# A feed-forward stage on one core: column tiles of the next chunk's first product between the pairs of the second, and more pairs by seven products

## The chip, the cores and the metric

The kernel runs on one core of one Trainium2 chip. The time is device microseconds of one launch; before the change the median of three runs was 1108.19 us (1107.41 to 1110.0). Smaller is better. The engines are PE (TensorE, the matrix unit; PEld is its weight load), DVE (VectorE), ACT (ScalarE), POOL (GpSimd) and SP (SyncE, which issues the transfers).

## The reference

One layer of an encoder: two batches of 128 tokens, width 2048. A mixer (two attentions and an output projection), a cross attention to a memory, and a feed-forward stage, each followed by a residual and a layer norm. The change lies wholly in the feed-forward stage:

```
def squared_relu_mlp(h, w_mlp_in, w_mlp_out):
    return jnp.square(jax.nn.relu(h @ w_mlp_in)) @ w_mlp_out

ff = squared_relu_mlp(x, w_mlp_in[l], w_mlp_out[l])
x = layer_norm(ALPHA * x + ff, ln3_g[l], ln3_b[l])
```

`w_mlp_in` is 2048 x 8192, `w_mlp_out` 8192 x 2048, all in fp32. The stage takes the time from about 400 us to 1096 us of the profiled execution.

## The kernel before

**Products in three.** Every fp32 operand is split into a part that the matrix unit takes at its reduced precision (hi) and the rest (lo): `split` lets ACT copy src to hi and DVE subtract to lo. A product is then three matmuls, hi x hi, hi x lo and lo x hi (`mm3`, lines 145 to 148). Weights come in blocks of 128 x 2048 fp32 (1 MB, "raw"), are split in parts of 1024 columns into buffers `w_hi` and `w_lo` (four of each), and are used once. So each part of weights costs one transfer, one ACT copy, one DVE subtraction, and the matmuls that read them.

**First product.** The 8192 hidden columns are four chunks of 16 tiles of 128. `hidden_group` makes four tiles at once in four PSUM banks: for each of 16 slices of the width, `cols_wide` issues four matmuls of 512 columns (weights hi times both parts of x, L195) and four of 256 (weights lo times x hi, L200). Per tile that is 16 of each. `hidden` and `square` evacuate the banks: ACT copies a half, DVE adds the other, takes relu and square in one operation (L823), and the result is split into `ht`.

**Second product.** The 2048 output columns are taken in two halves (q = 0, 1), so a chunk c has two passes (c, q). A pass accumulates over eight pairs of 128-row blocks of weights; the tokens are two blocks of 128. A plain pair is eight products (two row blocks, two column blocks of 512, two token blocks), 24 matmuls of 512 columns. A pair "by seven products" uses a Strassen-like identity in Winograd's form: 21 matmuls, for which DVE makes sums of the weight blocks (one operation over 1024 columns and two over 512, L886) and, once per chunk, sums of hidden blocks (four operations over 128 columns, then a split). The banks are x11, x12, x21, x22 and p1, p5, p6, p7; at the end of a pass they are combined and added to the residual `res` (L943, L946 from the banks, L949 from copies that ACT makes of the p banks). `SEVEN = ((2, 5, 7), (2, 5, 7))` names the pairs that go by seven. The last half pass, (3, 1), is plain and goes block by block (`proj_tokens` with `by_block`).

**Order.** A chunk's first product runs whole, then its two passes: the product of 16 tiles, 8 pairs, 8 pairs, next chunk. The program is written in Python in this order; a scheduler then sets each engine's order by dependence and priority, so engines may take work from a later place while buffers allow. Within an engine instructions run in the order that results. Side work (merges, statistics) stands in a queue `side`, of which `pump` takes an item after each part of weights. Weight sums stand in `sums`, taken in the same way, but the rest is flushed when the seven-product pair begins.

## Time and profile before

| | |
|---|---|
| median of three runs | 1108.19 us |
| profiled execution, span | 1106.6 us |
| mean granted PE clock | 0.997 |
| PE, DVE, ACT busy | 99%, 78%, 53% |
| first product of a chunk | 89.7 us |
| two passes of a chunk | 83.0 us |
| chunk 3's passes, the second plain | 86.0 us |
| after the last matmul | 10.5 us |

The time of a run is slightly more than the span, which begins with the first recorded instruction. A busy share is an average over the program. A line number stands for the code that issues an instruction, often a helper: L80 and L81 are the two operations of `split`, whoever calls it. The form `w_lo<-raw,w_hi 128x1024` names what is written and read, and the partitions and columns.

### The profile page before, as it was taken

How to read it: one execution, taken by the hardware profiler on the slowest of the kernel's cores; microseconds unless marked ns; L12 is line 12 of the kernel's file. 1: busy time of each engine (PE TensorE's matmuls, PEld its weight loads, DVE VectorE, ACT ScalarE, POOL GpSimd, SP SyncE). 2: the span in 40 equal slices, each digit the busy share in tenths (PEclk: the TensorE clock that was granted, in tenths of full speed). 3: DMA queues.
4: the chain of work that ended last, by engine and by line, in shares of the span. 5: the costliest groups of instructions: out<-in, count | busy, mean ns of one | idle time of the engine just before them, and what ended most of it. 6: DMA issues, size and time to landing. Idle time of an engine off the chain costs nothing.

```text
span 1106.6 us, 15304 instructions
## 1 busy us (share of the span) xinstructions
PE 1091.8 (99%) x5951; PEld 944.8 (85%) x5951; DVE 861.1 (78%) x1261; ACT 587.3 (53%) x860; POOL 35.6 (3%) x45
## 2 busy tenths in 40 slices
PE   9999999999999999999999999999999999999996
PEld 6988899988999878888888888888888888888885
DVE  6878677688879678888977678978668887678796
ACT  6455566545576435455655445555445555545550
POOL 1402000000100000000000000000000000000000
PEclk9999999999999999999999999999999999999998
DMA  9664453467567318744556555455554556555372
GB/s 333 234 227 142 156 193 127 174 220 247 180 205 272 145 44 299 266 166 181 192 223 221 184 185 209 181 200 192 198 183 175 204 200 223 186 191 190 115 255 87
DMA packets 37944, 215.86 MB, mean 195 GB/s; under 512 B 4336, under 2 KB 5232, under 8 KB 14192
## 3 DMA queue, kind: packets, MB, share of 16 engines
q1 hardware_dynamic: 37872, 214.89, 54.5%
q8 instruction: 46, 0.75, 0.3%
q14 instruction: 26, 0.21, 0.1%
HBM read 212.78 MB, written 2.10 MB: 194 GB/s over the span
## 4 chain that ended last, share of the span: by engine, by line
PE 98%; DVE 1%; DMA 0%; ACT 0%; issue 0%; POOL 0%; DVEq 0%; SPq 0%
PE acc L146 15%; PE acc L147 15%; PE acc L148 15%; PE acc L195 11%; PE att L195 11%; PE att L200 5%; PE acc L200 5%; PE att L147 3%; PE att L148 3%; PE att L146 3%; PE acc L188 2%; PE acc L186 2%; PE acc L187 2%; PE att L350 1%; PE acc L698 1%; PE att L528 1%
## 5 line engine op out<-in xcount | busy, mean ns | idle before, releaser
L81 DVE TENSOR_TENSOR w_lo<-raw,w_hi 128x1024 fp32r<-128x1024 f32 (+2 forms) x318 | 365.9, 1163 | 123.7 <-ACT w_hi L80 118.8
L80 ACT ACTIVATE w_hi<-raw 128x1024 fp32r<-128x1024 f32 (+2 forms) x318 | 317.9, 1011 | 266.0 <-PE acc L148 101.9
L80 ACT ACTIVATE w_hi<-wx 128x1024 fp32r<-128x1024 f32 x98 | 100.8, 1031 | 119.4 <-PE acc L148 85.5
L81 DVE TENSOR_TENSOR w_lo<-wx,w_hi 128x1024 fp32r<-128x1024 f32 x98 | 114.8, 1182 | 53.9 <-ACT w_hi L80 53.8
L195 PE MATMUL att<-x2t,w_hi 128*128 128x512 f32 x512 | 139.6, 394 | 0.0
L147 PE MATMUL acc<-w_lo,ht 128*128 128x512 f32 x354 | 137.8, 389 | 0.0
L148 PE MATMUL acc<-w_hi,ht 128*128 128x512 f32 x354 | 137.7, 389 | 0.0
L195 PE MATMUL acc<-x2t,w_hi 128*128 128x512 f32 x480 | 132.4, 394 | 0.0
L146 PE MATMUL acc<-w_hi,ht 128*128 128x512 f32 x354 | 111.5, 389 | 0.0
L195 PEld LDWEIGHTS att<-x2t,w_hi 128*128 128x128 f32 x512 | 88.0, 189 | 12.3
L195 PEld LDWEIGHTS acc<-x2t,w_hi 128*128 128x128 f32 x480 | 82.5, 189 | 11.5
L200 PEld LDWEIGHTS att<-x2t,w_lo 128*128 128x128 f32 x512 | 77.6, 189 | 10.3
L200 PEld LDWEIGHTS acc<-x2t,w_lo 128*128 128x128 f32 x480 | 73.3, 189 | 9.5
L200 PE MATMUL att<-x2t,w_lo 128*128 128x256 f32 x512 | 80.3, 281 | 0.0
L147 PEld LDWEIGHTS acc<-w_lo,ht 128*128 128x128 f32 x354 | 66.4, 188 | 14.0 <-DVE w_lo L81 0.2
L148 PEld LDWEIGHTS acc<-w_hi,ht 128*128 128x128 f32 x354 | 66.5, 188 | 13.8
L146 PEld LDWEIGHTS acc<-w_hi,ht 128*128 128x128 f32 x354 | 66.4, 188 | 13.8
L200 PE MATMUL acc<-x2t,w_lo 128*128 128x256 f32 x480 | 77.0, 281 | 0.0
L148 PE MATMUL acc<-w_hi,xt 128*128 128x512 f32 (+2 forms) x192 | 69.9, 365 | 0.0
L147 PE MATMUL acc<-w_lo,xt 128*128 128x512 f32 (+2 forms) x192 | 69.7, 364 | 0.0
L146 PE MATMUL acc<-w_hi,xt 128*128 128x512 f32 (+2 forms) x192 | 66.4, 366 | 0.8 <-ACT w_hi L80 0.8
L148 PE MATMUL acc<-w_hi,ot 128*128 128x512 f32 (+1 forms) x136 | 51.9, 382 | 0.0
(259 smaller groups left out, 1873.1 us busy)
## 6 DMA issues: line engine op xcount, KB each, us to landing
raw<-in_w_mi SPq DMA_DIRECT2D x64, 1024.0 KB, 4.9
wx<-in_w_mo SPq DMA_DIRECT2D x28, 1024.0 KB, 4.9
raw<-in_w_mo SPq DMA_DIRECT2D x28, 1024.0 KB, 4.8
raw<-in_w_out SPq DMA_DIRECT2D x16, 1024.0 KB, 4.9
raw<-in_w_ml SPq DMA_DIRECT2D x8, 1024.0 KB, 4.9
raw<-in_w_b SPq DMA_DIRECT2D x5, 1024.0 KB, 4.9
raw<-in_w_qa SPq DMA_DIRECT2D x16, 256.0 KB, 5.4
raw<-in_w_qa SPq DMA_DIRECT2D x4, 1024.0 KB, 4.8
```

The lines of the kernel that those rows point to most:

```text
L80: pin(nc.scalar.activation(hi, src, AF.Copy), pinned)
L81: return pin(nc.vector.tensor_tensor(out=lo, in0=src, in1=f(hi), op=ALU.subtract), pinned)
L146: nc.tensor.matmul(ps, ah, bh, start=start, stop=False)
L147: nc.tensor.matmul(ps, ah, bl, start=False, stop=False)
L148: nc.tensor.matmul(ps, al, bh, start=False, stop=stop)
L186: nc.tensor.matmul(ps, hi, xt[:, k, 0:S], start=k == 0, stop=False)
L187: nc.tensor.matmul(ps, hi, xt[:, k, S:2 * S], start=False, stop=False)
L188: nc.tensor.matmul(ps, lo, xt[:, k, 0:S], start=False, stop=k == nk - 1)
L195: pin(nc.tensor.matmul(ps, hi[:, i * P:(i + 1) * P], xt[:, k, :], start=k == 0, stop=k == nk - 1), pinned)
L200: pin(nc.tensor.matmul(ps[:, 0:S], lo[:, i * P:(i + 1) * P], xt[:, k, 0:S], start=False, stop=False), pinned)
L350: nc.tensor.transpose(pp[:, st * S + b * P:st * S + b * P + P], ev[:, b, st * P:(st + 1) * P], ident)
L528: nc.tensor.transpose(ps[:, o:o + P], x(b, k // 4)[:, (k % 4 + j) * P:(k % 4 + j + 1) * P], ident)
```

## The change

**Order of work.** Chunk 0's first product still runs whole, in groups of four tiles. From then on each pass alternates: one column tile ("g") of the next chunk's first product, then one pair of this pass. A pass with q = 0 carries six tiles, g,2,g,3,g,4,g,5,g,6,g,7,0,1; a pass with q = 1 ten: g before each of the pairs 2 to 7, and two before each of 0 and 1. A tile (`hidden_tile`) takes one 1 MB block of a new layout of the weights, `w_mc`, in two parts, and one bank: x22, which seven-product pairs do not use, or p6 at the start of a pass, or p1 and p7 by turns after the last seven-product pair. It issues eight matmuls of 512 columns and eight of 256 per part.

**Six of eight pairs by seven products.** In passes of chunks 0 to 2 pairs 2 to 7 go by seven, 0 and 1 are plain. Pass (3,0) has no tiles beside it and goes 0,4,1,5,2,6,3,7 with 4 to 7 by seven. Pass (3,1), no longer plain throughout, goes 0,5,6,1,7,2,3,4 with 5, 6, 7 by seven; the weights of the last three plain pairs are held, and their products with the second token block run at the very end, the last bank in two pieces of 256 columns.

**Evacuation.** Per tile one ACT copy and one DVE addition; per two tiles relu and square on ACT (L863, L864), one split of 512 columns and, where the pair goes by seven, the hidden sums. **Merges:** one ACT copy of p1 into `m_t`, then DVE adds p6, p7, and so on straight from the banks (L1036 to L1041), one at a time through a queue `banks` that `pump` serves first. Before the first seven-product pair of a pass what is left in `banks` is flushed. **Buffers:** weights in a ring of four blocks for both kinds; four fixed lo buffers `lo0` to `lo3`; one buffer `s_t` for weight sums instead of two; three instead of seven temporary buffers in this stage; hidden tiles of two chunks at once in `ht` and half of `aux`.

The diff, cut to its core:

```
-    SEVEN = ((2, 5, 7), (2, 5, 7))
+    SEVEN = (2, 3, 4, 5, 6, 7)
+    PASSES = [(c, q) for c in range(NCH) for q in range(2)]
+    ORDER = {cq: (2, 3, 4, 5, 6, 7, 0, 1) for cq in PASSES[:-2]}
+    SEVENS = {cq: SEVEN for cq in PASSES[:-2]}
+    ORDER[NCH - 1, 0], SEVENS[NCH - 1, 0] = (0, 4, 1, 5, 2, 6, 3, 7), (4, 5, 6, 7)
+    ORDER[NCH - 1, 1], SEVENS[NCH - 1, 1] = (0, 5, 6, 1, 7, 2, 3, 4), (5, 6, 7)
+    HELD = 3
+    FIRST = 6
...
+    def finish(h, c, p):
+        nc.scalar.activation(h, h, AF.Relu)
+        nc.scalar.activation(h, h, AF.Square)
+        take("h", c, p)
+        x = hid(c, p)
+        split(x[:, :, 0:S], x[:, :, S:2 * S], h.rearrange("p (i c) -> p i c", c=S))
+        if p in SEVEN:
...
+    for c, q in PASSES:
+        gs = [("g", c + 1, j) for j in range(CH)] if c < NCH - 1 else []
+        gs = gs[:FIRST] if q == 0 else gs[FIRST:]
+        us = [("u", c, q, p) for p in ORDER[c, q]]
+        n = len(gs) - len(us)
+        for i, u in enumerate(us):
+            twice = i >= len(us) - n if n > 0 else False
+            for _ in range(2 if twice else 1):
+                if gs:
+                    items.append(gs.pop(0))
+            items.append(u)
...
+    def hidden_tile(it, ps):
+        _, c, j = it
+        for h_ in range(2):
+            hi, lo = part(raw_of[it][:, h_ * 1024:(h_ + 1) * 1024])
+            k0 = 8 * h_
+            def w_hi(k):
+                nc.tensor.matmul(ps, hi[:, k * P:(k + 1) * P], x2t[:, k0 + k, :],
+                                 start=k0 + k == 0, stop=k0 + k == KT - 1)
+            for k in range(7):
+                w_hi(k)
+            if h_ == 0:
+                w_hi(7)
+            for k in range(8):
+                nc.tensor.matmul(ps[:, 0:S], lo[:, k * P:(k + 1) * P], x2t[:, k0 + k, 0:S],
+                                 start=False, stop=False)
+            if h_ == 1:
+                w_hi(7)
+        if j % 2 == 0:
+            lh[:] = [tmp_tile(), tmp_tile()]
+        evacuate(ps, *lh, j % 2)
+        if j % 2:
+            finish(lh[1], c, j // 2)
...
+                if n_seven == 0:
+                    while banks:
+                        banks.popleft()()
...
+                if n_seven == len(sevens):
+                    nc.scalar.activation(m_t, p1, AF.Copy)
+                    banks.extend([lambda: merge(r11, m_t), lambda: more(p6),
+                                  lambda: merge(r12, m_t, ALU.subtract), lambda: more(p7),
+                                  lambda: merge(r21, m_t), lambda: merge(r22, m_t, ALU.subtract),
+                                  lambda: merge(r22, p5), lambda: merge(r12, p5)])
```

**Where instructions move.** First DVE in the middle of a pass, before: `wx` and `raw` hold weight blocks and sums, L81 makes lo parts, L886 the weight sums; here a plain pair (6) and a seven-product pair (7) of one pass.

```order
L886 TENSOR_TENSOR wx_4178<-raw_6819 128x1024
L81 TENSOR_TENSOR w_lo_6719<-wx_4178,w_hi_6718 128x1024
L81 TENSOR_TENSOR w_lo_6730<-raw_6651,w_hi_6729 128x1024
L886 TENSOR_TENSOR wx_4178<-wx_4178,raw_6819 128x512
L81 TENSOR_TENSOR w_lo_6746<-raw_6651,w_hi_6745 128x1024
L886 TENSOR_TENSOR wx_4178<-wx_4178,raw_6819 128x512
L81 TENSOR_TENSOR w_lo_6763<-raw_6686,w_hi_6762 128x1024
L81 TENSOR_TENSOR w_lo_6773<-raw_6686,w_hi_6772 128x512
L81 TENSOR_TENSOR w_lo_6780<-wx_4178,w_hi_6779 128x1024
L946 TENSOR_TENSOR res1_1488<-res1_1488,acc_6502 128x512
```

And now, a column tile (weights in `raw_x`) and the seven-product pair after it (`raw_5011`); L88 makes lo parts, L919 the weight sums, L859 evacuates a tile, `aux` takes the split hidden values:

```order
L88 TENSOR_TENSOR lo3_4190<-s_t_4192,w_hi_5373 128x1024
L919 TENSOR_TENSOR s_t_4192<-s_t_4192,raw_5011 128x512
L88 TENSOR_TENSOR lo0_4187<-raw_x_4193,w_hi_5383 128x1024
L919 TENSOR_TENSOR s_t_4192<-s_t_4192,raw_5011 128x512
L88 TENSOR_TENSOR lo1_4188<-raw_x_4193,w_hi_5403 128x1024
L88 TENSOR_TENSOR lo2_4189<-raw_5011,w_hi_5429 128x1024
L88 TENSOR_TENSOR aux_4185<-tmp_5262,aux_4185 128x2x256
L88 TENSOR_TENSOR lo3_4190<-raw_5011,w_hi_5438 128x512
L88 TENSOR_TENSOR lo0_4187<-s_t_4192,w_hi_5444 128x1024
L919 TENSOR_TENSOR s_t_4192<-raw_5057 128x1024
L859 TENSOR_TENSOR tmp_5424<-acc_5052,tmp_5423 128x256
```

The sums of the next pair now stand between the lo parts of the tile and of the pair, in one buffer `s_t`, and evacuation and finishing of tiles stand there too.

Second, DVE at the start of pass (0,0): `tmp_5033` and `tmp_5042` are the last pair of chunk 0 (evacuated as a group), `tmp_5100` the first tile that ran alone, in bank `acc_5052` (x22); `raw_5057` and `s_t` belong to pair 3.

```order
L919 TENSOR_TENSOR s_t_4192<-s_t_4192,raw_5057 128x512
L88 TENSOR_TENSOR lo3_4190<-raw_5013,w_hi_5159 128x1024
L88 TENSOR_TENSOR lo0_4187<-raw_5057,w_hi_5187 128x1024
L919 TENSOR_TENSOR s_t_4192<-s_t_4192,raw_5057 128x512
L874 TENSOR_TENSOR tmp_5042<-tmp_5033 128x128 x2
L88 TENSOR_TENSOR lo1_4188<-raw_5057,w_hi_5196 128x512
L88 TENSOR_TENSOR ht_4184<-tmp_5033,ht_4184 128x2x256
L874 TENSOR_TENSOR tmp_5042<-tmp_5042,tmp_5033 128x128
L874 TENSOR_TENSOR tmp_5042<-tmp_5033,tmp_5042 128x128
L859 TENSOR_TENSOR tmp_5100<-acc_5052,tmp_5099 128x256
L88 TENSOR_TENSOR sums_x_4186<-tmp_5042,sums_x_4186 128x512
```

The tile's evacuation (L859) stands behind the lo parts of pair 3 and the finishing of the group; the next tile uses the same bank. Its matmuls on PE stand behind the first ones of pair 3, whose hi parts ACT makes from w_hi_5187 on:

```order
L153 MATMUL att_5053<-w_hi_5187,ht_4184 128x512
L153 MATMUL acc_5050<-w_hi_5187,aux_4185 128x512
L153 MATMUL acc_5049<-w_hi_5196,ht_4184 128x512
L154 MATMUL att_5053<-lo0_4187,ht_4184 128x512
L155 MATMUL att_5053<-w_hi_5187,ht_4184 128x512
L154 MATMUL acc_5050<-lo0_4187,aux_4185 128x512
L155 MATMUL acc_5050<-w_hi_5187,aux_4185 128x512
L154 MATMUL acc_5049<-lo1_4188,ht_4184 128x512
L155 MATMUL acc_5049<-w_hi_5196,ht_4184 128x512
L153 MATMUL att_5054<-w_hi_5202,aux_4185 128x512
L153 MATMUL att_5056<-w_hi_5202,aux_4185 128x512
L973 MATMUL acc_5052<-x2t_4038,w_hi_5139 128x512 x8
```

Third, DVE in the last pass: `att_5054` is bank p5, L1038 and L1041 merge the banks of pass (3,0), L507 are statistics of the residual, and the lo parts belong to pair 6 (`raw_5013`, `s_t`) and to the held weights of pair 2 (`wide`) of pass (3,1).

```order
L919 TENSOR_TENSOR s_t_4192<-raw_5013 128x1024
L88 TENSOR_TENSOR lo3_4190<-raw_5013,w_hi_9449 128x512
L1038 TENSOR_TENSOR res1_1491<-res1_1491,m_t_4191 128x512 x2
L88 TENSOR_TENSOR wide_9355<-raw_5011,wide_9355 128x1024 x2
L919 TENSOR_TENSOR s_t_4192<-s_t_4192,raw_5013 128x512
L507 BN_STATS bn_4183<-res1_1491 128x6
L1038 TENSOR_TENSOR res1_1491<-res1_1491,att_5054 128x512
L1038 TENSOR_TENSOR res0_1490<-res0_1490,att_5054 128x512
L919 TENSOR_TENSOR s_t_4192<-s_t_4192,raw_5013 128x512
L507 BN_STATS bn_4183<-res1_1491 128x6
L507 BN_STATS bn_4182<-res0_1490 128x6
L88 TENSOR_TENSOR lo0_4187<-s_t_4192,w_hi_9455 128x1024
```

The merges from p5 stand behind ten parts of the new pass, and the first matmuls that write p5 again stand on PE here (`w_hi_9418` and `w_hi_9455` are the weight sums of its first and second seven-product pair, 5 and 6):

```order
L154 MATMUL acc_5049<-lo3_4190,aux_4185 128x512
L155 MATMUL acc_5049<-w_hi_9449,aux_4185 128x512
L153 MATMUL att_5056<-w_hi_9455,aux_4185 128x512
L153 MATMUL att_5054<-w_hi_9418,aux_4185 128x512
L154 MATMUL att_5054<-lo0_4187,aux_4185 128x512
L155 MATMUL att_5054<-w_hi_9418,aux_4185 128x512
L153 MATMUL att_5054<-w_hi_9455,aux_4185 128x512
L153 MATMUL att_5055<-w_hi_9464,aux_4185 128x512
L153 MATMUL acc_5051<-w_hi_9464,aux_4185 128x512
```

So p5's product of the first seven-product pair comes after the other products of that pair and after the first parts of the next one.

More of the change, by code (lines that the diff above doesn't have):

```diff
@@ L826, in hidden @@
-    def hidden(ps, j):
-        r = []
-        for i in range(2):
-            r.append(square(ps[i]))
-            split(ht[:, j + i, 0:S], ht[:, j + i, S:2 * S], r[i])
-        if j // 2 in SEVEN[0]:
-            (a11, a21), (a12, a22) = [(x[:, 0:P], x[:, P:S]) for x in r]
+    aux = big.tile([P, 8192], F32R, tag="big", name="aux")
+    ht_x = aux[:, 0:4096].rearrange("p (k c) -> p k c", c=512)
+    sums_x = late.tile([P, 3072], F32R, name="sums_x")
+    sums_h = [aux[:, o:o + 1024] for o in range(4096, 8192, 1024)] + [
+        sums_x[:, o:o + 1024] for o in range(0, 3072, 1024)]
@@ new lines, in encoder_kernel, with take, give, hid @@
+    fixed = [late.tile([P, 1024], F32R, name=f"lo{i}") for i in range(4)]
+    m_t = late.tile([P, 512], F32, name="m_t")
+    s_t = late.tile([P, 2048], F32, name="s_t")
+    raw_x = late.tile([P, 2048], F32, name="raw_x")
+    fixed_lo.extend(fixed)
+    place, free = {}, {"h": list(range(12)), "s": list(range(7))}
+    def take(what, c, p):
+        place[what, c, p] = free[what].pop(0)
+    def give(what, c, p):
+        free[what].append(place[what, c, p])
+    def hid(c, p):
+        i = 2 * place["h", c, p]
+        return ht[:, i:i + 2, :] if i < CH else ht_x[:, i - CH:i - CH + 2, :]
@@ new lines, in part, with halves @@
+    def part(src, hi=None, lo=None):
+        w = src.shape[1]
+        if hi is None:
+            hi = wsp.tile([P, 1024], F32R, tag="w_hi", name="w_hi")
+        if lo is None:
+            lo = lo_tile()
+        split(hi[:, :w], lo[:, :w], src)
+        if banks:
+            pump()
+        if sums:
+            sums.popleft()()
+        else:
+            pump()
+        return hi[:, :w], lo[:, :w]
+    def halves(hl):
+        hi, lo = hl
+        return [(hi[:, o:o + 512], lo[:, o:o + 512]) for o in range(0, hi.shape[1], 512)]
@@ new lines, in one_pass @@
+                n_seven += 1
+                if at[0] < len(items) and is_seven(items[at[0]]):
+                    push_sums(items[at[0]])
+                if n_seven == len(sevens):
[4 more added lines that the diff above has]
+                                  lambda: merge(r22, p5), lambda: merge(r12, p5)])
+            elif final and len(order) - n_unit < HELD:
+                n = len(parts) // 2
+                for i in range(2):
+                    o = (2 * n + i) * 1024
+                    lo = wide[:, 6144 + o:7168 + o] if n == 0 else aux[:, 2048 + o:3072 + o]
+                    w = halves(part(raw[:, i * 1024:(i + 1) * 1024], wide[:, o:o + 1024], lo))
+                    parts.append((k + i, w))
+                    for (hi, lo), ps in zip(w, (x12, x11)):
+                        mm(ps, a(c, k + i, 0), hi, lo)
@@ L931, in pair_product @@
             else:
                 for i in range(2):
-                    w = part(raw[:, i * 1024:(i + 1) * 1024])
+                    w = halves(part(raw[:, i * 1024:(i + 1) * 1024]))
                     for (hi, lo), to in zip(w, ((x12, x22), (x11, x21))):
                         for b in range(2):
-                            ah, al = a(k + i, b)
-                            mm3(to[b], ah, al, hi, lo, p == 0 and i == 0, to[b] is x22 and p == plain[-1] and i == 1)
-        cols = [slice((2 * q + i) * 512, (2 * q + i + 1) * 512) for i in range(2)]
@@ L997, in encoder_kernel @@
-    g3, b3 = raw_tile(), raw_tile()
+                            mm(to[b], a(c, k + i, b), hi, lo)
+            if q == 1:
+                give("h", c, p)
+                if p in SEVEN:
+                    give("s", c, p)
+        if not final:
+            for r, ps in ((r22, x22), (r12, x12), (r11, x11), (r21, x21)):
+                merge(r, ps)
+            if c == NCH - 1:
+                banks.extend([lambda b=b, r=r: stats(sts[b], r)
+                              for b, r in ((0, r11), (0, r12), (1, r21), (1, r22))])
+            return
@@ new lines, in one_pass, with done @@
+        pump(len(banks))
+        merge(r22, x22)
+        def done(b, r, ps):
+            nc.vector.tensor_tensor(out=r, in0=r, in1=ps, op=ALU.add)
+            stats(sts[b], r)
+        done(0, r12, x12)
+        done(0, r11, x11)
+        for ps, i, r, pieces in ((x21, 1, r21, ((0, 512),)), (x22, 0, r22, ((0, 256), (256, 256)))):
+            for c0, w in pieces:
+                to, part_r = (ps if w == 512 else pt[c0 // w])[:, :w], r[:, c0:c0 + w]
+                for n, (k, hl) in enumerate(parts):
+                    hi, lo = [x[:, c0:c0 + w] for x in hl[i]]
+                    if w == 512:
+                        mm(ps, a(c, k, 1), hi, lo)
+                    else:
+                        mm3(to, *a(c, k, 1), hi, lo, n == 0, n == len(parts) - 1)
+                done(1, part_r, to)
```

278 lines of the change are left out of this document (138 added, 140 removed).

## Prediction

> **What bounds the kernel now.** I read the page first: the busy line and the chain that ended last.
>
> ```profile
> span 1106.6 us, 15304 instructions
> PE 1091.8 (99%) x5951; PEld 944.8 (85%) x5951; DVE 861.1 (78%) x1261; ACT 587.3 (53%) x860; POOL 35.6 (3%) x45
> PE 98%; DVE 1%; DMA 0%; ACT 0%; issue 0%; POOL 0%; DVEq 0%; SPq 0%
> ```
>
> TensorE (PE) is the chain, and DVE, at 78%, is the next engine. An average over the program says little about one stage, so the windows are cut at the stage borders of the MLP: first product of chunk 1, its two passes, the last half-pass, and the tail.
>
> ```profile
> core 0: us, PE busy (x) PEld busy (x) DVE busy (x) ACT busy (x) POOL busy (x), PEclk, DMA share, GB/s
> 575.00:664.70 89.70, 89.70 (x513) 78.45 (x512) 63.53 (x94) 44.16 (x63) 0.00 (x0) 1.00 0.57 197
> 664.70:747.70 83.00, 83.00 (x368) 68.72 (x367) 71.67 (x89) 47.44 (x59) 0.00 (x0) 1.00 0.52 193
> 1010.10:1096.10 86.00, 85.98 (x424) 72.75 (x422) 69.20 (x94) 39.06 (x47) 0.91 (x1) 1.00 0.46 163
> 1096.10:1106.60 10.50, 0.00 (x0) 0.00 (x0) 6.84 (x14) 0.00 (x0) 0.92 (x1) 0.63 0.27 101
> ```
>
> PE has no idle time in any of these stretches, at a granted clock of 1.00. A matmul less is a gain as long as DVE and ACT keep ahead. In the passes DVE fills 71.67 of 83.00 us (86%). The waits say how it stands with its partners:
>
> ```profile
> ACT w_hi L80 <- PE acc L148: 187.4, 148, 4.5
> DVE w_lo L81 <- ACT w_hi L80: 172.6, 147, 5.0
> ```
>
> ACT waits for PE to free a weight buffer and DVE waits for ACT, on average 1.2 us each time: today both are ahead of PE. The change spends this lead.
>
> **What is removed.** Seven passes are 7 x (5 x 24 + 3 x 21) = 1281 matmuls of 512 columns, and the last half-pass 192 equivalents, 1473 in all. Now six passes are 2 x 24 + 6 x 21 = 174, pass (3,0) has 4 x 24 + 4 x 21 = 180 and (3,1) 5 x 24 + 3 x 21 = 183: 1407, or 66 fewer. A pass pair of 366 took 83.00 us, 0.2268 us each, so 15.0 us go. The last stretch (375 equivalents, 85.1 us by that rate) took 0.9 us more because 96 of its products are 256-column pieces; the new end has 36, which saves 0.6.
>
> A column tile of the first product keeps its 16 x 512 and 16 x 256 columns, but issues eight of a kind in a row to one bank, where four banks took four of a kind each.
>
> ```profile
> 774.44 0.93 PE att L195 x4
> 790.80 0.96 PE att L200 x8
> 691.23 0.39 PE L146 MATMUL att<-w_hi,ht 128*128 128x512 f32 x1
> 692.81 0.39 PE L147 MATMUL acc<-w_lo,ht 128*128 128x512 f32 x1
> ```
>
> Four 512s take 0.93 (0.2325 each), eight 256s 0.96; the seven of the second product between the last two rows are 0.226 apart. A tile costs 89.70 / 16 = 5.61 us now. If eight in a row reach 0.2268 it costs 16 x (0.2268 + 0.118) = 5.52; if nothing changes, 5.61. Over 48 tiles that is 0 to 4.3 us; I take 3, nearer the second product's rows, whose matmuls also stay in a bank.
>
> **What is added to DVE.** Its spacing when it never waits:
>
> ```profile
> 693.88 1.23 DVE L81 TENSOR_TENSOR w_lo<-raw,w_hi 128x1024 fp32r<-128x1024 f32 x1
> 695.02 0.68 DVE L886 TENSOR_TENSOR wx<-wx,raw 128x512 f32<-128x512 f32 x1
> 695.62 1.22 DVE L81 TENSOR_TENSOR w_lo<-raw,w_hi 128x1024 fp32r<-128x1024 f32 x1
> 645.99 0.42 DVE L81 TENSOR_TENSOR ht<-tmp,ht 128x256 fp32r<-128x256 f32 x1
> 646.33 0.28 DVE L838 TENSOR_TENSOR tmp<-tmp 128x128 f32<-128x128 f32 x1
> 646.53 0.42 DVE L81 TENSOR_TENSOR ht<-tmp,ht 128x256 fp32r<-128x256 f32 x1
> ```
>
> So 1.14 us for 1024 columns, 0.60 for 512, 0.34 for 256, 0.20 for 128. A seven-product pair has 3 x 1.14 + 0.60 of splits and 1.14 + 2 x 0.60 of weight sums: 6.36 us, against 21 x 0.2268 = 4.76 on PE. A plain pair: 2.28 against 5.44. A column tile: 2 x 1.14 + 0.34 = 2.62 against 5.55. Each pair of tiles is finished with 0.60, and 1.4 more where it has hidden sums. A pass merges with 12 x 0.60 (before as now, 12).
> Per chunk: DVE 12 x 6.36 + 4 x 2.28 + 16 x 2.62 + 8 x 0.60 + 6 x 1.4 + 24 x 0.60 = 155 us, PE 16 x 5.55 + 348 x 0.2268 = 168. DVE goes from 135 of 172.7 (78%) to 92%. One tile plus one seven-product pair is 8.98 on DVE, with finishing on average 9.8, against 10.3 on PE. ACT, at 1.06 per 1024 (rows below), stays under 70%.
>
> ```profile
> L80 ACT ACTIVATE w_hi<-raw 128x1024 fp32r<-128x1024 f32 x280 | 293.6, 1060 | 246.4 <-PE acc L148 85.9 <-PE acc L195 66.9 <-PE att L195 52.2
> L821 ACT ACTIVATE tmp<-att 128x256 f32<-128x256 f32 x32 | 10.0, 382 | 13.2 <-PE att L195 13.2
> L954 ACT ACTIVATE tmp<-att 128x512 f32<-128x512 f32 x28 | 15.8, 590 | 0.0
> L946 DVE TENSOR_TENSOR res<-res,acc 128x512 f32<-128x512 f32 x20 | 13.3, 680 | 1.2 <-PE acc L148 1.2
> ```
>
> In the steady cycle I walked the order with these durations. The next tile's accumulator waits for the last tile's evacuation (ACT 0.39, DVE 0.34) but one whole pair lies between, 4.76 us, and four weight parts are buffered ahead; no stall comes out, with 2 us to spare. Relu and square go to ACT, which has the room. Three places have no such cover:
>
> *Start of pass (0,0).* Chunk 0's last two pairs are still to be evacuated and finished when the first tile runs and pairs 2 and 3 (both seven-product) follow. PE has 5.55 + 4.76 + 11 x 0.2268 = 12.8 us of work until tile 1 needs x22 back. DVE's rows up to that evacuation (6 of 1024 columns, 7 of 512, 5 of 256, 8 of 128) add to 6.84 + 4.2 + 1.7 + 1.6 = 14.3 us, begin 1.0 after the group's end and wait, walked step by step, 1.1 for ACT, which is itself behind: 16.4. Loss 3.6, and 0.4 at the next split: 4.0 (2.5 if DVE never waits, 5 if it waits twice as long).
>
> *Change of pass, q 0 to q 1,* three times: the first plain pair's lo part stands behind the new pair's sum, which waits for its transfer of 4.8 us. 0.3 each, 0.9 (0 to 2.4).
>
> *Last pass.* No tiles run there. The eight bank merges and four statistics that pass (3,0) leaves all stand, in DVE's order, among the splits of its first two seven-product pairs, and p5, merged last, is needed by the first of them. DVE begins that stretch 0.5 us before PE ends pass (3,0). Its rows up to the merge of p5: 8 x 1.14 and 2 x 0.60 of splits, 2.34 of sums, 9 merges and 2 statistics of 0.60: 19.3 us, so p5 is free 18.8 us after that end. PE has 52 matmuls ahead of p5, 11.8 us. Loss 7.0, and 0.5 more where weight sums of that pair are late: 7.5 (5 to 8.5).
>
> *Clock.* A wait of 5 us in one piece can cost clock:
>
> ```profile
> 1096.10:1098.00 1.90, 0.00 (x0) 0.00 (x0) 1.78 (x5) 0.00 (x0) 0.34 (x1) 1.00 0.00 0
> 1098.00:1100.00 2.00, 0.00 (x0) 0.00 (x0) 2.00 (x4) 0.00 (x0) 0.57 (x1) 0.73 0.00 0
> 1100.00:1102.00 2.00, 0.00 (x0) 0.00 (x0) 2.00 (x5) 0.00 (x0) 0.00 (x0) 0.50 0.48 188
> ```
>
> About 3 us after its last matmul PE is at 0.50 (1.00, then 0.73, then 0.50). How long it would stay there with work no row shows; if as long as it took to fall, 3 us of work at half speed lose 1.5. I take 0.5 for the one wait that is long enough, as the next weights are late there anyhow (0 to 1.5).
> The Trainium skill, page "TensorE: Matmul & The Clock Gate", Part 1 on the clock gate, says an idle window of about 3.4 us halves the clock and about 3.4 us of sustained work restores it; the tail's 3 us agrees with the first half, no run here shows the second, and by the rule an estimate of the loss would be 1.7 us.
>
> The tail after the last matmul (10.5 us) ends, as before, with a 256-column piece, statistics and the scaling: nothing.
>
> **Sum.** -15.0 - 0.6 - 3.0 + 4.0 + 0.9 + 7.5 + 0.5 = -5.7 us, on the profiled 1106.6: 1100.9. The runs' median, 1108.19, is 1.6 above the profiled span; so 1102.5.
>
> **Rivals.**
> *PE never waits.* Both stalls rest on my reading of how far DVE is ahead; in every window above PE waits for nothing, and DVE has a 1.2 us wait to give away each time. Then 1108.2 - 18.6 plus a microsecond or two: about 1090 to 1096. Against it: 19.3 us of DVE rows stand before p5 whatever the lead. 22%.
> *The forecast,* 1097 to 1106: 40%.
> *Gain and stalls cancel.* No rate gain in the first product (+3) and stalls at their upper ends (+1.0, +1.5, +1.0, +1.0): 7.5 more, 1110, or anything from 1106 on. 15%.
> *DVE becomes the bound, slower.* In order, DVE cannot fill a wait for ACT with other work. A chunk has 168 - 155 = 13 us of slack for 12 cycles of pair and tile, 1.1 us each. The mean wait before is 1.2; it was harmless because DVE was ahead. If a cycle forces 1.5 us (a sum waits for its transfer, and the splits behind it wait as well), 0.4 x 36 = 14 us are lost: 1116. It is slower than before from about 1.3 us per cycle. For it: DVE at 92%, only one buffer for weight sums (two before). Against: four weight parts ahead, and waits that overlap PE's own. 23%.
>
> The predicted time is the forecast's, 1102.5, its own range 1097 to 1106. To leave out no more than two in ten, the range takes in most of the first and half of the last case: 1090 to 1113. A difference under 0.2% (2.2 us) can't be told from none here: faster (under 1106.0) 0.62, same 0.15, slower 0.23.
>
> **What would show it.** In the changed profile PE busy should be near 1091.8 - 18.6 = 1073, with idle time of PE in three places: a few waits of about 1 us in the first 25 us after chunk 0's first product, and one of about 5 us some 15 us into the last pass, where the row of att (p5) waits for DVE's res<-res,att. A column tile should take 5.5 to 5.6 us. DVE should be busy 92% of chunks 1 to 3. It is wrong if PE waits in every cycle of tile and pair (DVE the bound), if the long wait at p5 is missing (DVE further ahead than walked), or if tiles take over 5.65.

## The result, and the profile after

The change made the kernel slower: 1119.26 us, median of four runs, against 1108.80 beside it, a ratio of 1.0096 with a 95% interval of [1.0082, 1.0110]. The forecast was 1102.5, with a range of 1090 to 1113: the sign and the range were wrong.

The profiled execution has a span of 1117.1 us (1106.6 before). Its busy line and its chain of waits:

```profile
span 1117.1 us, 15372 instructions
PE 1085.0 (97%) x5855; PEld 930.1 (83%) x5855; DVE 949.0 (85%) x1344; ACT 641.6 (57%) x928; POOL 38.2 (3%) x45
PE 88%; DVE 6%; DMA 2%; ACT 1%; issue 1%; SPq 0%; POOL 0%; DVEq 0%; ACTq 0%
```

PE has 96 instructions less, as the change says, and a chain that was 98% PE now holds 6% of DVE. The windows, cut at the new stages (pass (0,1), and the same passes of chunks 1 and 2 are alike; the middle of the last pass; its rest; what follows the last matmul), say where:

```profile
core 0: us, PE busy (x) PEld busy (x) DVE busy (x) ACT busy (x) POOL busy (x), PEclk, DMA share, GB/s
565.60:661.40 95.80, 95.11 (x492) 80.77 (x491) 91.32 (x122) 57.52 (x75) 0.00 (x0) 1.00 0.58 204
1064.00:1069.00 5.00, 0.20 (x2) 0.17 (x2) 5.00 (x8) 0.00 (x0) 0.00 (x0) 0.82 0.00 0
1069.00:1101.70 32.70, 32.59 (x149) 26.81 (x149) 27.28 (x37) 10.82 (x12) 0.00 (x0) 0.92 0.36 129
1101.70:1117.10 15.40, 0.00 (x0) 0.00 (x0) 12.05 (x25) 0.00 (x0) 1.83 (x2) 0.60 0.36 137
```

DVE is 95% busy in a whole pass with PE at 99%: the steady alternation works. But there is a hole of almost 5 us in the last pass, a lower granted clock in and behind it (0.82, 0.92), and 15.4 us after the last matmul where there were 10.5.

The timeline of PE gives each wait, in brackets, with what ended it. These are the longest of every place:

```profile
506.50 0.51 PE L154 MATMUL acc<-lo,ht 128*128 128x512 f32 x1 [0.40 <-DVE lo L88]
515.94 0.50 PE L154 MATMUL att<-lo,aux 128*128 128x512 f32 x1 [0.55 <-DVE lo L88]
560.03 0.50 PE L154 MATMUL acc<-lo,ht 128*128 128x512 f32 x1 [0.55 <-DVE lo L88]
639.99 1.19 PE L973 MATMUL att<-x2t,w_hi 128*128 128x512 f32 x4 [0.45 <-DVE m_t L1041]
753.30 0.50 PE L153 MATMUL att<-w_hi,aux 128*128 128x512 f32 x1 [0.24 <-ACT w_hi L87]
901.90 0.50 PE L154 MATMUL acc<-lo,ht 128*128 128x512 f32 x1 [1.41 <-DVE lo L88]
1062.97 0.50 PE L154 MATMUL acc<-lo,aux 128*128 128x512 f32 x1 [0.54 <-DVE lo L88]
1068.84 0.79 PE L153 MATMUL att<-w_hi,aux 128*128 128x512 f32 x1 [4.80 <-DVE res L1038]
```

To compare terms I took the start-to-start distance of all matmuls of the stage and subtracted, for each, the distance that its kind had before (512 columns of the second product 0.2267, of the first 0.2320, 256 columns 0.119). What is left over 0.05 us is counted as a wait, so a stretch at a lower granted clock is in the waits too:

| part of the sum | forecast | measured |
|---|---|---|
| fewer matmuls and pieces | -15.6 | -15.3 |
| rate of the column tiles | -3.0 | -1.9 |
| start of pass (0,0) | +4.0 | +3.9 |
| changes of pass, three of each kind | +0.9 | +7.4 |
| last pass, the clock with it | +8.0 | +10.0 |
| after the last matmul | 0 | +5.0 |
| second product, each matmul a little later (0.2276) | 0 | +1.2 |
| stage begins later, rest | 0 | +0.2 |
| total | -5.7 | +10.5 |

### The profile page after: what moved, and what is told of

It is laid out like the page before. It is cut to its first block, busy times and chain, and to the rows that moved or that the text cites. A ratio compares the mean times of both kernels' runs of the same rounds, so it can differ in the third digit from the quotient of the medians.

```text
span 1117.1 us, 15372 instructions
## 1 busy us (share of the span) xinstructions
PE 1085.0 (97%) x5855; PEld 930.1 (83%) x5855; DVE 949.0 (85%) x1344; ACT 641.6 (57%) x928; POOL 38.2 (3%) x45
## 4 chain that ended last, share of the span: by engine, by line
PE 88%; DVE 6%; DMA 2%; ACT 1%; issue 1%; SPq 0%; POOL 0%; DVEq 0%; ACTq 0%
PE acc L154 12%; PE acc L155 12%; PE acc L153 12%; PE acc L973 9%; PE att L973 6%; PE acc L981 5%; PE att L153 4%; PE att L154 4%; PE att L155 4%; PE att L981 3%; PE acc L202 3%; PE att L202 3%; PE acc L195 2%; PE acc L193 2%; PE acc L194 2%; DVE lo L88 2%
## 5 line engine op out<-in xcount | busy, mean ns | idle before, releaser
L88 DVE TENSOR_TENSOR lo<-raw,w_hi 128x1024 fp32r<-128x1024 f32 (+1 forms) x190 | 206.5, 1101 | 8.7 <-ACT w_hi L87 7.7
L88 DVE TENSOR_TENSOR w_lo<-raw,w_hi 128x1024 fp32r<-128x1024 f32 (+2 forms) x130 | 146.0, 1132 | 59.2 <-ACT w_hi L87 58.2
L88 DVE TENSOR_TENSOR lo<-s_t,w_hi 128x1024 fp32r<-128x1024 f32 x86 | 104.9, 1221 | 18.4 <-ACT w_hi L87 13.2
L87 ACT ACTIVATE w_hi<-s_t 128x1024 fp32r<-128x1024 f32 x86 | 90.7, 1056 | 42.5 <-PE acc L155 24.6
L973 PE MATMUL att<-x2t,w_hi 128*128 128x512 f32 x272 | 70.4, 393 | 1.3 <-DVE m_t L1041 1.3
L981 PEld LDWEIGHTS acc<-x2t,lo 128*128 128x128 f32 x496 | 67.6, 190 | 4.7
L981 PE MATMUL acc<-x2t,lo 128*128 128x256 f32 x496 | 69.1, 282 | 0.0
L88 DVE TENSOR_TENSOR lo<-raw_x,w_hi 128x1024 fp32r<-128x1024 f32 (+1 forms) x56 | 66.7, 1209 | 2.7 <-ACT w_hi L87 2.6
L154 PE MATMUL acc<-lo,ht 128*128 128x512 f32 x158 | 62.0, 392 | 2.4 <-DVE lo L88 2.4
L155 PE MATMUL acc<-w_hi,ht 128*128 128x512 f32 x158 | 61.6, 390 | 0.0
L919 DVE TENSOR_TENSOR s_t<-s_t,raw 128x512 f32<-128x512 f32 x84 | 57.4, 684 | 0.1
L153 PE MATMUL acc<-w_hi,ht 128*128 128x512 f32 x158 | 54.9, 396 | 0.3 <-ACT w_hi L87 0.3
L919 DVE TENSOR_TENSOR s_t<-raw 128x1024 f32<-128x1024 f32 x42 | 51.3, 1222 | 1.5 <-DMA raw<-in_w_mo 0.8
```

What stands on the lines that cost most here:

```text
L87: pin(nc.scalar.activation(hi, src, AF.Copy), pinned)
L88: return pin(nc.vector.tensor_tensor(out=lo, in0=src, in1=f(hi), op=ALU.subtract), pinned)
L153: nc.tensor.matmul(ps, ah, bh, start=start, stop=False)
L154: nc.tensor.matmul(ps, ah, bl, start=False, stop=False)
L155: nc.tensor.matmul(ps, al, bh, start=False, stop=stop)
L919: sums.append(lambda: nc.vector.tensor_tensor(out=out, in0=a, in1=b, op=ALU.add))
```

## The experiments

All are versions of the changed kernel. "Waits" are found as above, from one profiled execution each; the tail is the distance from the start of the last matmul to the end of the span (10.8 before, 15.8 after the change).

| run | median us | ratio to the kernel before | waits in the last pass | tail |
|---|---|---|---|---|
| the change | 1119.26 | 1.0096 [1.0082, 1.0110] | 10.0 | 15.8 |
| e1, two tiles first | 1116.26 | 1.0058 [1.0043, 1.0073] | 10.1 | 15.3 |
| e2, plain pairs end (3,0) | 1116.68 | 1.0059 [1.0042, 1.0076] | 8.1 with (3,0) | 15.0 |
| e3, last pass plain | 1109.63 | 0.9995 [0.9985, 1.0004] | 0.2 | 14.1 |
| e4, three sevens | 1122.46 | 1.0116 [1.0098, 1.0134] | 11.3 | 15.5 |
| e5, p5 merged first | 1119.76 | 1.0085 [1.0068, 1.0102] | 9.7 | 16.1 |
| e6, end in program order | 1117.75 | 1.0069 [1.0054, 1.0084] | 12.2 | 11.8 |
| e7, p6 not p7 | 1116.25 | 1.0062 [1.0046, 1.0078] | 9.6 | 15.6 |
| e8, e1 + e3 + e6 | 1105.32 | 0.9960 [0.9946, 0.9975] | 0.2 | 11.8 |
| e9, no weight sums last | 1113.64 | 1.0034 [1.0024, 1.0044] | 5.0 | 14.7 |
| e10, lo in program order | 1395.95 | 1.2578 [1.2549, 1.2606] | (all over) | 18.4 |
| e11, e8 + e7 | 1103.49 | 0.9942 [0.9920, 0.9963] | 0.2 | 11.8 |
| e12, e11 + e10 | 1372.29 | 1.2357 [1.2328, 1.2385] | (all over) | 11.8 |
| e13, sum after plain pairs | 1120.66 | 1.0091 [1.0077, 1.0105] | 9.8 | 15.8 |
| e14, (3,0) plain | 1115.92 | 1.0051 [1.0034, 1.0068] | 5.1 | 15.1 |
| e15, e11 + e13 | 1104.18 | 0.9942 [0.9929, 0.9955] | 0.2 | 11.8 |

Medians of the kernel before, taken beside these runs, lie up to 1.4 us apart (1108.80 to 1110.22), so gains of 1 us are read from the waits.

### Is the start its own cost? (e1)

```
-            twice = i >= len(us) - n if n > 0 else False
+            twice = i >= len(us) - n if n > 0 else (c, q, i) == (0, 0, 0)
...
-                    ps = x22 if (c, q) == (0, 0) else p6
+                    ps = x22 if it == ("g", 1, 0) else p6
```

> Only the first pass differs: it begins with two column tiles (banks x22 and p6) instead of one, and has none between the pairs 6 and 7. Theory A (the wait at the start is the evacuation and finishing of chunk 0's last group, which a second tile of 5.6 us covers): the 3.9 us of waits in the first 25 us after chunk 0's first product fall to 0.5 or less, some 1.6 us may come back where two seven-product pairs follow each other (6.36 us on DVE against 4.76 on PE), so 1119.3 becomes 1116 to 1117. Theory B (DVE is short over the whole pass, the place is an accident): the waits only move to later pairs of the pass, 1119 as before.

The 3.9 us of waits at the start are gone entirely: in the first 25 us of the pass no row of PE has a bracket. 1.5 us come back between pairs 6 and 7, where the tile is missing, and 1.3 more in the next pass, while 1.7 go at two changes of pass. Over the whole stage the waits fall from 21.3 to 18.6, and the median by 3.0. That is theory A, with part of the gain moved: a second tile, 5.6 us of PE and 2.6 of DVE, is enough cover for the group's finishing, and the place that it left has less.

### The last pass: order or amount? (e2, e5, e9, e14)

e2 changes one table and lets (3,0) end with two plain pairs:

```
-    ORDER[NCH - 1, 0], SEVENS[NCH - 1, 0] = (0, 4, 1, 5, 2, 6, 3, 7), (4, 5, 6, 7)
+    ORDER[NCH - 1, 0], SEVENS[NCH - 1, 0] = (4, 0, 5, 1, 6, 7, 2, 3), (4, 5, 6, 7)
```

> Pass (3,0) goes 4,0,5,1,6,7,2,3, so that its last seven-product pair is followed by two plain pairs before the last pass begins, and DVE can merge the banks there (a plain pair leaves it 3.2 us). Theory A (p5's merge is late because it stands behind the new pass's splits): the wait of 4.8 us at p5 falls below 1 us, the clock stays at 1.00 there, the last pass loses 2 to 3 us instead of 10, and 1 to 2 us come back where 6 and 7 follow each other; the tail stays at 15 us: 1112 to 1114. Theory B (DVE simply has more to do than PE over both last passes): the waits move into pass (3,0), 1117 to 1120.

The wait in one piece is gone and the granted clock stays at 1.00, as A said. But waits of up to 1.3 us appear in the last pass and short ones in (3,0), 8.1 us in all, 1.1 of them in (3,0), and the time, 1116.7, lies next to B's. Of the change's 10.0 us some 2.4 are matmuls at half clock, so 7.6 are waits proper: e2 has no fewer of them, and its gain is the clock. Here are the longest, from the timeline of PE in e2:

```profile
1053.20 0.50 PE L154 MATMUL att<-lo,ht 128*128 128x512 f32 x1 [1.28 <-DVE lo L88]
1062.69 0.50 PE L153 MATMUL att<-w_hi,aux 128*128 128x512 f32 x1 [0.54 <-ACT w_hi L87]
1067.77 0.74 PE L153 MATMUL att<-w_hi,aux 128*128 128x512 f32 x2 [1.11 <-ACT w_hi L87]
1071.85 0.50 PE L153 MATMUL att<-w_hi,aux 128*128 128x512 f32 x1 [0.58 <-ACT w_hi L87]
```

e5 leaves the work where it is and moves p5's merges from last to second in pass (3,0):

```
-                                  lambda: merge(r21, m_t), lambda: merge(r22, m_t, ALU.subtract),
-                                  lambda: merge(r22, p5), lambda: merge(r12, p5)])
+                    p5s = [lambda: merge(r22, p5), lambda: merge(r12, p5)]
...
+                    banks.append(lambda: merge(r11, m_t))
+                    banks.extend(p5s + p67 if c == NCH - 1 else p67 + p5s)
```

> Only the order of the merges of pass (3,0) differs: those from p5 come right after the first, not last. Theory A (the 4.8 us wait is p5's place in a queue): by DVE's rows p5 is free some 4 us after the pass begins and p7, now the last one that PE needs, 14.7 us after, where PE comes to it at 12 to 14: a wait of 1 to 2 us in place of 4.8, too short for the clock to fall, so the last pass loses 4 to 6 us instead of 10: 1114 to 1115. Theory B (DVE is short of time over the last two passes whatever the order, as moving the plain pairs suggested): 1117 to 1119, with the waits spread out.

B, though in one piece and not spread out. The wait only changes its name: at nearly the same place PE now waits for the lo part of the next pair's weight sums, again over 4 us.

```profile
1068.39 0.39 PE L153 MATMUL att<-w_hi,aux 128*128 128x512 f32 x1
1072.86 0.50 PE L154 MATMUL att<-lo,aux 128*128 128x512 f32 x1 [4.07 <-DVE lo L88]
```

DVE's own timeline in e5 shows no idle time there, and what it does meanwhile:

```profile
1066.31 0.69 DVE L1041 TENSOR_TENSOR m_t<-m_t,att 128x512 f32<-128x512 f32 x1
1066.91 0.69 DVE L507 BATCH_NORM_STATS2 bn<-res 128x6 f32<-128x512 f32 x1
1067.51 2.35 DVE L88 TENSOR_TENSOR wide<-raw,wide 128x1024 fp32r<-128x1024 f32 x2
1069.77 0.69 DVE L919 TENSOR_TENSOR s_t<-s_t,raw 128x512 f32<-128x512 f32 x1
1070.37 1.29 DVE L1038 TENSOR_TENSOR res<-res,m_t 128x512 f32<-128x512 f32 x2
1071.58 1.22 DVE L88 TENSOR_TENSOR lo<-s_t,w_hi 128x1024 fp32r<-128x1024 f32 x1
```

Statistics, and the splits of the held pair 2 (`wide`), which PE first reads at 1084.3, stand ahead of the lo part that it waits for. So the amount decides, and part of the amount ahead is not urgent.

e9 leaves out the last pass's weight sums, with old sums multiplied in their place, and e14 the merges that (3,0) leaves. The edits are, in e9, that `push_sums` is not called for the last pass, at two places, of which this is one:

```
-                if at[0] < len(items) and is_seven(items[at[0]]):
+                if at[0] < len(items) and is_seven(items[at[0]]) and items[at[0]][1:3] != PASSES[-1]:
```

and in e14 `SEVENS[NCH - 1, 0] = ()`.

> The weight sums of the last pass's three seven-product pairs are left out (stale sums are split and multiplied in their place, so the output of that half is not the reference's): 7.0 us of DVE less, all matmuls, merges, splits and transfers as in the change. Theory B (DVE's throughput over the last pass sets the wait, whatever stands first): 2.3 us of these stood ahead of p5's merge, so the wait of 4.8 us falls to about 2.5, the clock stays up, and the last pass loses 4 to 6 us instead of 10: 1113 to 1115. Rival (the wait belongs to the merges alone, or to ACT): 4.5 us or more remain, 1118 to 1119.

> Pass (3,0) is plain throughout (12 more matmuls, 2.7 us), the last pass keeps its three seven-product pairs. So no merges from p banks are left for the last pass, while its weight sums stay. Theory A (the wait at p5 is the merges of (3,0) plus the sums of (3,1) plus splits, all on DVE): without the merges (8 x 0.60 us) the wait at p5 is gone, since p5 is free from the start; the last pass loses 1 to 4 us instead of 10; the tail stays at 15 to 16: 1113 to 1116. Rival (the sums and splits of the last pass alone are too much): 5 us or more are lost there, 1117 to 1119.

In e9 the wait at p5 shrinks from 4.80 to 1.21, more than the 2.3 us of sums that stood ahead of it, and the pass loses 5.0, with the clock at 1.00. In e14 p5 never waits, and 5.1 are lost at the lo parts. That is above theory A's 1 to 4 and just in the rival's range (5 or more), though the time, 1115.9, is in A's (1113 to 1116): some 1.4 of the 5.1 are again matmuls at half clock, and the other 3.7 are waits of the sums and splits alone. So both halves of the work hold PE up. The longest rows of PE, e9 and then e14:

```profile
1067.36 0.50 PE L153 MATMUL att<-w_hi,aux 128*128 128x512 f32 x1 [1.21 <-DVE res L1038]
```

```profile
1068.31 0.51 PE L154 MATMUL acc<-lo,aux 128*128 128x512 f32 x1 [1.76 <-DVE lo L88]
```

The last pass is short of DVE: it has the merges of the pass before, the sums and the splits at once, and no tile's 5.6 us of PE beside them.

### The last pass without its seven-product pairs (e3)

```
-    ORDER[NCH - 1, 1], SEVENS[NCH - 1, 1] = (0, 5, 6, 1, 7, 2, 3, 4), (5, 6, 7)
+    ORDER[NCH - 1, 1], SEVENS[NCH - 1, 1] = (0, 5, 6, 1, 7, 2, 3, 4), ()
```

> The last pass (3,1) has no seven-product pairs: 9 more matmuls of 512 columns (+2.0 us), and no p banks to wait for or to merge at the end. Theory A (the last pass's 10 us and the 5 us by which the part after the last matmul grew both come from the p banks there): last pass 1 us of waits, 10.5 us after the last matmul, 1119.3 - 9 - 5 + 2 = 1107. Rival (the tail grew for another reason, the block-by-block end and the held weights): the tail stays at 14 to 15 us and the time is 1111 to 1112.

Nine more matmuls, 2.0 us, and yet 9.6 us faster: the three seven-product pairs of that pass cost far more than they save. The waits are as theory A has them (0.2), the tail as the rival does: it stays at 14.1. The time, 1109.6, lies between the two forecasts. So a second thing is wrong there.

### Why the end is longer (e6)

DVE before, around the last matmul (it ends at 1096.1):

```profile
1085.93 0.69 DVE L994 TENSOR_TENSOR res<-res,att 128x512 f32<-128x512 f32 x1 [4.95 <-PE att L148]
1093.24 0.42 DVE L500 BATCH_NORM_STATS2 bn<-res 128x6 f32<-128x256 f32 x1
1093.58 0.47 DVE L1014 SCALAR_TENSOR_TENSOR res<-res,rs_r,raw 128x256 f32<-128x256 f32 x1
1096.12 0.42 DVE L994 TENSOR_TENSOR res<-res,att 128x256 f32<-128x256 f32 x1 [2.08 <-PE att L148]
```

The first token block is complete at 1085.9, 10.2 us before the end of the last matmul. It is normalised and scaled (L1006, L1014), and DVE idle for 2.08 us, before the last piece comes. After the change (last matmul ends at 1101.7):

```profile
1090.84 0.69 DVE L1041 TENSOR_TENSOR m_t<-m_t,att 128x512 f32<-128x512 f32 x1 [4.66 <-PE att L155]
1101.62 0.42 DVE L1111 TENSOR_TENSOR res<-res,att 128x256 f32<-128x256 f32 x1
1102.03 1.41 DVE L1145 SCALAR_TENSOR_TENSOR res<-res,mv,s_t 128x512 f32<-128x512 f32 x2
1107.25 0.48 DVE L1153 SCALAR_TENSOR_TENSOR res<-res,rs_r,raw_x 128x256 f32<-128x256 f32 x1
```

Until 1090.84 DVE is idle for 4.66 us, waiting for the bank of the last seven-product pair; behind that stand seven of the eight merges, and the first block's scaling begins only at 1102.0, after the last matmul. In e3 there are no such merges, but x11 and x12, the first block's banks, are complete only at 1088.5, 6.8 us before the end of the last matmul (1095.3), because the order on PE puts products of the second block between theirs. The row of e3 on which DVE takes them, and that of e6 below, whose last matmul ends at 1104.3:

```profile
1088.53 1.37 DVE L1111 TENSOR_TENSOR res<-res,acc 128x512 f32<-128x512 f32 x2 [7.70 <-PE acc L155]
1095.29 1.37 DVE L1111 TENSOR_TENSOR res<-res,acc 128x512 f32<-128x512 f32 x2 [1.55 <-PE acc L155]
```

e6 keeps the held products in written order:

```
+                        mm(ps, a(c, k + i, 0), hi, lo, True)
...
+                        mm(ps, a(c, k, 1), hi, lo, True)
...
+                        mm3(to, *a(c, k, 1), hi, lo, n == 0, n == len(parts) - 1, True)
```

where the last argument keeps these instructions in the order of the program.

> The held pairs' products are kept in the order in which they are written: x11 and x12 first, then the second token block (x21, x22). Theory A (the tail grew because the first token block is done 3 us before the last matmul, and its statistics and scaling, 8 us of DVE, lie behind the end): x11 and x12 end 8.4 us before the last matmul, the part after it falls from 15.8 to 12 or 13, and the last pass may lose up to 2 us more where PE now waits for lo parts: 1115 to 1119. Rival (the tail grew because the merges of the last pass's p banks are late): the tail stays at 15 to 16 us.

Theory A for the tail: it falls from 15.8 to 11.8, with the first block complete 9.0 us before the end of the last matmul. In the windows (the last row is what follows the last matmul):

```profile
1064.50:1104.40 39.90, 32.87 (x150) 25.97 (x149) 36.92 (x52) 10.82 (x12) 0.91 (x1) 0.91 0.33 121
1104.40:1115.90 11.50, 0.00 (x0) 0.00 (x0) 8.02 (x18) 0.00 (x0) 0.92 (x1) 0.60 0.35 131
```

But the waits grow by 2.2 us, as PE now waits for parts of the last seven-product pair instead of doing products of the second block meanwhile. Alone it gains little; without those pairs nothing is given back, and the tail is the same 11.8 (e8). So in this order the merges add nothing to it, and the 1.0 over the 10.8 of before stands beside a first block that is complete 1.2 us later; that this is its cause was not tried.

### The changes of pass (e4, e7, e13)

e4 keeps the alternation and goes back to three seven-product pairs per pass, `SEVEN = (2, 5, 7)`, plain pairs last, with two in the last pass.

> The alternation stays, but only pairs 2, 5, 7 go by seven products as before the change (5 and 7 in the last pass): 60 more matmuls of 512 columns than the change, 13.6 us, and 12 us less DVE work per pass. Theory A (the steady alternation costs nothing, the loss is at the pass starts and at the end): start and last pass lose about the same as with six (3 and 5 to 8 us), the middle 3 to 5 us less: 1124 to 1130, slower than the change. Theory B (the alternation is fine but six sevens overload DVE throughout): the waits go to nearly nothing and the tail back to 10.5, so about 1108.

Theory A in its sign, with a time just under its range. B is right on the waits in the middle, where between 510 and 1000 us there is not one over 0.05 us, and wrong on the tail (15.5) and the time. Alternation is free, and so are the changes of pass when DVE has 12 us less to do per pass. The start still loses 1.6 us. The last pass loses 11.3 all the same, some of it in 10.2 us at half clock (1074.9 to 1085.1), and 60 more matmuls cost 13.6 us.

With six there are three waits at each chunk. The first is before q goes from 0 to 1 (0.8, 0.8 and 1.7 us). On DVE, in the third of them:

```profile
898.03 0.68 DVE L1038 TENSOR_TENSOR res<-res,m_t 128x512 f32<-128x512 f32 x1
899.48 1.23 DVE L919 TENSOR_TENSOR s_t<-raw 128x1024 f32<-128x1024 f32 x1 [0.77 <-DMA raw<-in_w_mo]
900.62 1.22 DVE L88 TENSOR_TENSOR lo<-raw_x,w_hi 128x1024 fp32r<-128x1024 f32 x1
```

The next pass's first sum waits for its transfer, and the lo part that PE needs is behind it. In the other two the sum (at 557.62 and 728.13) stands ahead of the lo part too, but waits for nothing, and the wait is half as long. e13 puts this sum after the plain pairs' lo parts, and nothing else:

```
+        late = it[2] == 1 and it[3] == 2 and it[1] < NCH - 1
...
+            sums.append(lambda: pin(nc.vector.tensor_tensor(out=out, in0=a, in1=b, op=ALU.add), late))
```

(and the same for the lo parts of plain pairs of these passes).

> In the three passes with q = 0 of chunks 0 to 2, the first weight sum of the next pass stands on DVE after the lo parts of the plain pairs 0 and 1 instead of ahead of them; nothing else is fixed. Theory A (the 0.8, 0.8 and 1.7 us before the change of q are this sum standing first, and its wait for the transfer): these waits go, 3.3 us, unless the sum is then late for pair 2 of the next pass, where at most 1 us each comes back: 1116 to 1118. Rival (DVE is late there by the amount of work): the waits stay or move, 1119.

The three waits are gone, 3.3 us, and the waits at the pass that follows go from 0.63 to 2.17 each, 4.6 us: the sum is late there instead. A row of PE in e13, where 0.24 stood:

```profile
581.33 0.50 PE L153 MATMUL att<-w_hi,aux 128*128 128x512 f32 x1 [0.88 <-ACT w_hi L933]
```

So the place was right and its removal no gain: 1.5 us come back each time where A allowed 1, and the time, 1120.7, is the change's within the spread of the medians. The third kind of wait, at 639.99, is a tile that waits for the merge of p7. e7 gives it p6, merged two places earlier (`spare = spare or [p1, p6]`).

> After the last seven-product pair the tiles take the banks p1 and p6 by turns instead of p1 and p7. Theory (the wait of 0.45 us, 0.7 with its ramp, in the three passes with q = 1 is the tile waiting for the merge of p7, which stands fourth in the queue; p6 stands second): these three waits go, 2.1 us, 1117.2. Rival: DVE is late there anyway, and the wait moves to the next lo part: 1119.

These three waits, 2.2 us, are gone and don't come back elsewhere.

### A fixed order on DVE (e10, e12)

```
+        pin(nc.vector.tensor_tensor(out=lo[:, :w], in0=src, in1=f(hi[:, :w]), op=ALU.subtract), True)
...
+            sums.append(lambda: pin(nc.vector.tensor_tensor(out=out, in0=a, in1=b, op=ALU.add), True))
```

> On DVE the lo parts and the weight sums stand in the order in which they are written, in all passes. So sums of the next pass no longer stand ahead of the lo part of pair 0 that PE waits for, and in the last pass the splits of the held pair 2 (2.3 us) no longer stand ahead of the sums of pair 6. Theory A (work that is not urgent is put first): the three waits of 0.8 to 1.7 us before the change from q = 0 to q = 1 fall to under 0.3, 3 us, and the last pass loses 6 to 8 us instead of 10: 1113 to 1115. Rival (DVE's amount of work counts, not its order): the waits move, 1118 to 1120.

> The same with lo parts and weight sums on DVE in the order in which they are written. Theory A: the waits before the change of q (0.8, 2.0) go as well: 1100 to 1102. Rival: the fixed order takes away freedom that the steady cycle needs, new waits there, 1104 or more.

In e10 neither theory: 26% slower, with the same work. In e12 (24%) the rival's sign, new waits in the steady cycle, far beyond its size. From the page of e10, and its waits:

```profile
PE 1169.1 (84%) x5855; PEld 980.1 (70%) x5855; DVE 953.3 (68%) x1344; ACT 659.3 (47%) x928; POOL 38.3 (3%) x45
DVE tmp L859 <- ACT tmp L858: 200.0, 46, 8.4
PE att L153 <- ACT w_hi L931: 148.4, 38, 6.5
```

DVE is busy for the same 950 us. PE is busy for 84 us more (1085.0 in the change), at a mean granted clock of 0.911 where the change has 0.991, so part of the loss is clock that falls in the waits. DVE now waits 200 us for ACT in front of the tiles' evacuation, with splits of the next pairs behind it. In its order the evacuation of a tile stands five lo parts and sums earlier than in the change, ahead of the parts that PE needs before that tile. This is the mechanism of the rival "DVE becomes the bound", a DVE that stands in its order: it exists, and here it costs 276 us of the span with the clock that falls. That the position of the evacuation alone makes it was not tried.

### The three together (e8, e11, e15)

> Two tiles first in (0,0), no seven-product pairs in the last pass, and the end in program order. If the causes are separate, the gains of the first two (3.5 and 10.3 us by the medians) add, and the third brings the tail of 14.1 to 12: 1119.3 - 3.5 - 10.3 - 2 = 1103.5, or 0.5% faster than before. If they share one cause (DVE short of time), less than the sum: 1106 to 1108.

> The three together (two tiles first, plain last pass, end in program order) and p6 in place of p7. The waits of 0.7 us at q = 1 go where they still stood (two of three): 1105.3 - 1.5 to 2.5 = 1103 to 1104, 0.5 to 0.6% faster than before.

> The best version so far (two tiles first, plain last pass, end in program order, p6 in place of p7) with the sum after the plain pairs. Theory A: 4 to 5 us of waits before the change of q go, 1103.5 - 3 to 4 = 1100, 0.9% faster than before. Rival: 1103 to 1104.

e8 has its sum nearly in full, 13.9 of 15.8 us: 1105.3, between the 1103.5 for separate causes and the 1106 to 1108 for a shared one, so the causes are separate in the main. With p6 in place of p7 (e11) 1103.5, a ratio of 0.9942 [0.9920, 0.9963]: faster than both kernels. That p6 adds to e8 is not shown: the two intervals overlap, and both profiled executions have 10.0 us of waits, as in e11 the waits at p7 are gone but one of 2.17 stands before the last change of q, with half clock behind it. e15's trace has fewer waits (7.5 us), but its time is the same, as its rival said. In e15, the whole stretch from the first pass to the last chunk, the last chunk, and what follows:

```profile
492.00:1000.00 508.00, 504.01 (x2563) 427.30 (x2562) 471.10 (x610) 316.02 (x413) 0.00 (x0) 1.00 0.54 197
1000.00:1089.10 89.10, 89.03 (x409) 74.00 (x407) 74.14 (x93) 39.52 (x44) 0.91 (x1) 1.00 0.48 173
1089.10:1100.60 11.50, 0.00 (x0) 0.00 (x0) 8.01 (x18) 0.00 (x0) 0.92 (x1) 0.61 0.35 131
```

DVE at 93% beside a PE that hardly waits.

## Why the prediction was wrong

The forecast missed by 16.2 us, from -5.7 to +10.5: 6.5 at the changes of pass, 5.0 after the last matmul, 2.0 in the last pass, and 2.7 in the rates of the two products (1.1 and 1.2) and small terms.

**The step that failed in kind is "The tail after the last matmul (10.5 us) ends, as before ...: nothing".** It looked at the kind of the last instructions, not at what DVE still had to do when they began. The first block's normalisation had been hidden under the second block's products; with fewer of these, in another order, and eight merges from the last seven-product pair, 5.0 us of it came out. e6 took 4.0 of them back by PE's order alone, with the merges still there. e3, without merges and with PE's order left as it was, took back 1.7. Together (e8) they take no more than e6, so the order is the larger part, and 1.0 stays open.

**Changes of pass, "0.3 each, 0.9 (0 to 2.4)": 7.4.** This is the largest miss. The first kind was seen at the right place, the lo part behind the new pair's sum, and sized at 0.9 where it measured 3.3, above the upper end of 2.4; the sum's wait for its transfer is in the trace at one of the three only. Two kinds were not seen, the pair at a pass's start (1.9) and the tile behind p7's merge (2.2). With three seven-product pairs and plain pairs last all of them are gone (e4). e13 speaks for DVE's amount of work at the first place, since the wait came back elsewhere when the position was changed; e7 shows that the p7 part was one bad position.

**Last pass, 7.5 and 0.5: 10.0.** The wait at p5 was rightly placed and named (5 us some 15 us into the pass; 4.80 measured, from 14 us on). All waits there come to some 7.6, and the agreement with 7.5 is partly luck: the walk gave p5 7.0, which cost 5.1, and another 2.1 were lost ahead of it, where the walk had 0.5. The clock was undersized: some 2.4 us, above the upper end of 1.5. The prediction took what stood ahead of p5's merge in the queue as the price; e5 shows that moving the merge forward doesn't lower it, and e9 and e14 that less work does.

**Tile rate, -3.0: -1.9.** The 512-column matmuls of the tiles are 0.229 apart (0.232 before), where a gain of 3.0 needs about 0.228; the 256-column ones did not gain (0.1185 and 0.119). The second product's own went from 0.2267 to 0.2276 between waits, 1.2 us in all, which no term had and no run explains.

**Right:** the matmuls saved (15.6 and 15.3), the start (4.0 and 3.9, confirmed by e1), and that the steady cycle holds with DVE at 93% (451.90 of 487.20 us from 516.0 to 1003.2): in pass (0,1) nothing waits between 583.6 and 639.1. The sign "PE busy near 1073" failed (1085.0): a matmul behind a wait, or at half clock, is longer in the trace, so part of the lost time counts as busy.

**The rivals.** "DVE becomes the bound" gave 1116 and 23%, nearest to the result, but its place was the cycle of tile and pair, where nothing waits, so the nearness is luck. Waits for DVE stood at the starts and ends of the passes. "Gain and stalls cancel" had the right kind of case with bounds too small: the terms at the edges were sized one by one, and the tail was in none of them.

The sum was also too fine for its base: terms of -18.6 and +12.9, where each stall was bounded by walking my own order of events. A loss of 5 us in a place that was not walked at all is the larger kind of error.

## What to carry to other kernels

Costing matmuls is easy and was right to 0.3 us; a change that fills a second engine from 78% to over 90% is decided at the places where its cover ends: the first tile, each change of pass, the last pass and what is left for that engine after the last matmul. For each such place add up that engine's work from the point where it can begin to the point where it is needed, and see what no longer lies under the other's work. When a wait is removed by moving one instruction, look at whether the engine is idle there: where it is not, the wait may only change its name, as in e5 and e13.
